# One bias table for the edge blocks, read at offsets, with the row minimum taken in two steps

## The chip, the cores and the metric

The kernel runs on one core of a Trainium2 chip. The metric is device time in microseconds (us), the median of several executions; before the change it is 943.72 us over 3 executions (942.9 to 944.77). One execution was recorded by the hardware profiler, and all durations below come from it.

Engine names: PE is the matrix engine, PEld its weight loads, DVE the vector engine, ACT the scalar engine, POOL the GpSimd engine, SP the engine that issues the DMAs here. DMAs are issued in order from SP's queue.

## The reference: what is computed

One layer of an encoder block over 2 sequences (256 and 2048 tokens of 1024 numbers), with the same 16 learned meta tokens ahead of each. All in float32:

- h = rmsnorm(z), then one projection h @ w_in into q (8 heads of 64), k and v (2 key/value heads), an attention gate, and the value, gate and output gate of a convolution group.
- The convolution group: a gated product, a depthwise convolution of width 31, a layer norm over channels, SiLU.
- The attention group: each real query sees all 16 meta keys without a distance penalty, and the real keys at distance up to 128 with the penalty slope × distance (ALiBi); every softmax row has a learned sink logit besides.
- out = z + concat(attention × SiLU(gate), convolution × SiLU(gate)) @ w_out; the meta tokens are dropped from the output.

The part that the change touches is the score of a block of queries:

```
s = (q @ k^T) * scale - slope * |t - s|      # real keys within 128, else -inf
s_meta = (q @ k_meta^T) * scale              # no penalty
p = softmax([sink, s_meta, s])
```

The row's maximum (here: the minimum of the negated scores, with the negated sink as the starting value) is needed before the exponential.

## The kernel before, in words

Tokens are cut into 18 blocks of 128 (blocks 0 and 1 are the short sequence, 2 to 17 the long one). The work runs in two stages that overlap at their border.

**Projection, norm, convolution (to about 605 us).** PE multiplies in float32r with operands split in a high and a low part, three passes for each product (`proj_et` L856 and `proj_te` L873). The convolution's taps run on DVE. `ln_block` (L211) does the layer norm of the convolution for one block: PE transposes (`lnt`), DVE takes statistics and writes the tile `zn` (L234), PE transposes back (`lnu`, L240), ACT applies SiLU into `zn` (L243), and a DMA stores `zn` as `cd` (L246). `zn` has three buffers, so the write at L234 waits until the store of three blocks ago has landed.

**Attention and output projection.** `attention_open` (L255) allocates a pool on the right side of the on-chip memory. In it are `bias` (128 partitions × 2 × 3040 bf16 before), two key windows `kw`, three score tiles `sb`, the value tiles, `q` (two buffers before) and `q2`. It loads `q` of block 0, the keys, the bias table (L269) and the values. From there the work is cut in slots: `slot_step` (L625), eight slots for each block. In slot 0 of block a the `q` and keys of block a+1 are loaded (`load_q` L327, `load_k` L295), in slot 3 its values; in slot 6 `q_prep` (L392) transposes the `q` of block a+1 on PE (tile `qT`) into `q2`. Each slot has one `scores` (L410), for a key/value head kv and a quarter n of 32 queries × 4 heads:

- PE: two matmuls into the PSUM tile S (L427);
- one slot later `bias_max` (L434): DVE adds the bias to S, writes `sb` and takes the row minimum into a column of `nm`, in one tensor_tensor_reduce (L441), which the profile shows as a CUSTOM_DVE_ANT_0 and a DVE_READ_ACCUMULATOR2_ANT. POOL clears the columns of `sb` that this quarter does not see (L440);
- two slots later `expo`: ACT takes the exponential with `nm` as its offset (L453);
- three slots later, for n = 3, `norm`: DVE forms the reciprocal sums (`es`, L465 and L466), POOL multiplies `sb` by them (L470 for the meta columns of edge blocks, L479).

In the next eight slots `bank` (L491) transposes `sb` on PE (tiles pT_c, pT_m, pT_x), ACT and DVE split it (L515, L516), `pv` multiplies by the values (tile O, L533), `merge` joins and gates the halves (L555 to L566, tile `rest`). `outproj` (L601) does the output projection, six matmuls of 512 columns in each slot (L609), and `yo` is added and stored.

A block is of one of three kinds (L290). Blocks 0 and 2 are "first", 1 and 17 are "last"; these four are the edge blocks, whose window lacks one side. The other 14 are "in". SPANS (L61) gives the columns that a quarter uses: 304 or 336 of an "in" block, 176, 208, 240 and 272 for the four quarters of an edge block. Before, KEYS and BIAS_AT (L66 to L76) lay out one stretch of the bias table for each kind and quarter: 1248 columns for "in", 896 for "first", 896 for "last", 3040 in all, with zeros under the meta keys.

**What sets the order.** The kernel gives a program order, with work put off by so many slots (`later`, `tick`). `TileContext(schedule_with_timeline_sim=True)` (L1310) lets the framework choose the order on each engine's queue from its own estimate of the times. From `attention_open` on, POOL keeps the program order (MAN1, L261); from `attention_rest` (L679) on, PE does too (MAN2, L683). SP, ACT and DVE stay with the framework throughout. The first 14 slots, block 0 and six slots of block 1, run among the last 18 q projections (`spread`, L658), where PE's order is the framework's too. Waits between engines, and for buffers that are used again, are put in by the framework.

Of the kernel before, what the change touches and what calls it, by code (L numbers as in the profile page):

```python
# [11 lines left out]
F32 = mybir.dt.float32  # L12
# [3 lines left out]
ALU = mybir.AluOpType  # L16
AX = mybir.AxisListType

P = 128
D = 1024  # L20
ND = D // P
NM = 16
# [14 lines left out]
BIG = 1.0e30  # L37
# [20 lines left out]
QB = 32  # L58
QC = P // 2
LA, MA, CC, LB, RA, MB, RB, KW = 0, 64, 80, 208, 272, 336, 352, 416  # L60
SPANS = {  # L61
    "in": ((LA, RA + QB), (LA + QB, MB), (CC, RB + QB), (CC, KW)),
    "first": tuple((MA, LB + QB * (n + 1)) for n in range(4)),
    "last": tuple((CC + QB * n, RB) for n in range(4)),
}
KEYS = {  # L66
    "in": ((LA, MA, -P), (MA, CC, None), (CC, LB, 0), (LB, RA, QC - P), (RA, MB, P), (MB, RB, None), (RB, KW, P + QC)),
    "first": ((MA, CC, None), (CC, MB, 0)),
    "last": ((CC, MB, -P), (MB, RB, None)),
}  # L70
BIAS_AT = {}
BIAS_N = 0
for _kind, _spans in SPANS.items():
    for _n, (_c0, _c1) in enumerate(_spans):
        BIAS_AT[_kind, _n] = BIAS_N - _c0
        BIAS_N += _c1 - _c0  # L76
XR = QC + NM
PIN_X = 7
PIN_W = 2
# [20 lines left out]
def hymba_kernel(  # L100
# [11 lines left out]
    nc = tc.nc  # L112
# [22 lines left out]
    snk, msk, nsnk = vec[:, 22:24], vec[:, 24:28], vec[:, 28:30]  # L135
# [26 lines left out]
    def later(k, f):  # L162
        due.setdefault(clock[0] + k, []).append(f)
# [86 lines left out]
    pool, cst, kw, wo, wo_slot, sbs = {}, {}, [], {}, {}, []  # L250
    vt, qt, q2t, sbt, pmt, gat, gct, cnt, mix, att, yot, opj = ({} for _ in range(12))
# [38 lines left out]
    def kind(b):  # L290
        return "first" if b in (0, NB_P) else "last" if b in (NB_P - 1, NB - 1) else "in"

    vt, qt, q2t, sbt, pmt, gat, gct, cnt, mix, att, yot, opj = ({} for _ in range(12))
# [31 lines left out]
        nc.sync.dma_start(t[3][NM:XR], vd[b + 1, QC:P])  # L325

    def load_q(b):  # L327
        qt[b] = pool["a"].tile([P, 4, P], F32, tag="q", name=f"q{b}")
        nc.sync.dma_start(qt[b].rearrange("p a e -> p (a e)"), qd[b])

    def presplit_wo(e):
# [48 lines left out]
    def pin(on):  # L380
        def wrap(f):
            def g(*a, **k):
                r = f(*a, **k)  # L383
                if on:
                    tc.keep_in_program_order(r)
                return r

            return g

        return wrap  # L390
# [19 lines left out]
    def scores(b, kv, n):  # L410

        c0, c1 = SPANS[kind(b)][n]
        w = c1 - c0
        if n == 0:
            sbt[b, kv] = sbs[(2 * b + kv) % 3]
            stat[b, kv] = (
                pool["a"].tile([P, 4], F32, tag="nm", name=f"nm{b}_{kv}", bufs=3),
                pool["a"].tile([P, 4], F32, tag="rs", name=f"rs{b}_{kv}", bufs=3),
                pool["a"].tile([P, 4], F32, tag="es", name=f"es{b}_{kv}", bufs=3),
            )  # L420
        sb = sbt[b, kv]
        nm, rs, es = stat[b, kv]
        ps = psum.tile([P, 512], F32, tag="a", name=f"S{b}_{kv}_{n}")
        for hl_k in range(2):
            pin(b == 0 and hl_k == 0)(
                nc.tensor.matmul)(
                ps[:, 0:w],  # L427
                q2t[b][:, n, 2 * kv : 2 * kv + 2].rearrange("p a c q -> p (a c q)"),
                kw[b % 2][:, kv, hl_k, c0:c1],
                start=(hl_k == 0),  # L430
                stop=(hl_k == 1),
            )

        def bias_max():  # L434
            at = BIAS_AT[kind(b), n]
            z0, z1 = {"in": (0, 0), "first": (c1, MB), "last": (CC, c0)}[kind(b)]
            if n == 0 and b == NB_P + 1:
                z0, z1 = c1, MB
            if z1 > z0:
                nc.gpsimd.memset(sb[:, n, z0:z1], 0.0)  # L440
            nc.vector.tensor_tensor_reduce(  # L441
                out=sb[:, n, c0:c1],
                in0=ps[:, 0:w],
                in1=cst["bias"][:, kv, at + c0 : at + c1],
                scale=1.0,
                scalar=nsnk[:, kv : kv + 1],
                op0=ALU.add,
                op1=ALU.min,
                accum_out=nm[:, n : n + 1],
            )  # L450

        def expo():
            nc.scalar.activation(  # L453
                sb[:, n, c0:c1],
                sb[:, n, c0:c1],
                AF.Exp,
                bias=nm[:, n : n + 1],
                scale=-1.0,
                accum_out=rs[:, n : n + 1],
            )  # L460
            if n == 3:
                nc.scalar.activation(es, nm, AF.Exp, bias=snk[:, kv : kv + 1])

        def norm():
            nc.vector.tensor_tensor(es, es, rs, op=ALU.add)  # L465
            nc.vector.reciprocal(es, es)  # L466
            if kind(b) != "in":
                pm = pool["a"].tile([P, 2, 4, NM], F32, tag="pm", name=f"pm{b}_{kv}", bufs=1)
                at = MA if kind(b) == "first" else MB
                nc.gpsimd.tensor_tensor(  # L470
                    pm,
                    sb[:, :, at : at + NM].unsqueeze(1).to_broadcast([P, 2, 4, NM]),
                    es.unsqueeze(1).unsqueeze(3).to_broadcast([P, 2, 4, NM]),
                    op=ALU.mult,
                )
                pmt[b, kv] = pm
            for k in range(4):
                a0, a1 = SPANS[kind(b)][k]
                nc.gpsimd.tensor_scalar(  # L479
                    sb[:, k, a0:a1], sb[:, k, a0:a1], es[:, k : k + 1], 1.0, op0=ALU.mult, op1=ALU.mult  # L480
                )

        later(1, bias_max)
        later(2, expo)
        if n == 3:
            later(3, norm)
# [214 lines left out]
    if True:  # L701
# [491 lines left out]
        for i, (c, u, g) in enumerate(items):  # L1193
# [25 lines left out]
            for k in loads.get(i, []):  # L1219
# [3 lines left out]
                for q in range(4):  # L1223
                    at = max(1, min(room, W0 + q * min(WST, max(1, (room - 2) // 4))))
# [27 lines left out]
def layout(inputs):  # L1252
    f = {k: np.asarray(v) for k, v in inputs.items()}
    z = np.concatenate([f["meta_tokens"], f["x_prompt"][0], f["x_sample"][0]], axis=0)
    zt = np.ascontiguousarray(z.T).reshape(ND, P, COLS)
    w = f["w_in"][0]
    q, k, v, ga, cv, cg, gc = np.split(w, np.cumsum([512, 128, 128, 512, 512, 512])[:6], axis=1)
    units = []
    for j in range(NJ):
        units.append(np.concatenate([cg[:, P * j : P * j + P], cv[:, P * j : P * j + P]], axis=1))  # L1260
    units += [gc[:, :UW], gc[:, UW:], q[:, :UW], q[:, UW:], np.concatenate([k, v], axis=1), ga[:, :UW], ga[:, UW:]]
    w_in = np.stack([u.reshape(ND, P, UW).transpose(1, 0, 2) for u in units])
    col = lambda a, n: a.reshape(n, P).T
    vecs = np.concatenate(
        [
            col(f["norm_w"][0], 8),
            col(f["conv_b"][0], 4),
            col(f["conv_ln_w"][0], 4),
            col(f["conv_ln_b"][0], 4),
            np.tile(f["q_norm_w"][0], 2)[:, None],  # L1270
            np.tile(f["k_norm_w"][0], 2)[:, None],
        ],
        axis=1,
    )
    conv_w = f["conv_w"][0].reshape(TAPS, NJ, P).transpose(2, 1, 0)
    row = np.arange(P)
    local = row // QB
    sink = np.stack([f["sink_logits"][0][4 * kv + local] for kv in range(KV)], axis=1)
    slopes = np.exp2(-8.0 * np.arange(1, H + 1, dtype=np.float32) / H).astype(np.float32)
    bias_c = np.zeros((P, KV, BIAS_N), np.float32)  # L1280
    for kv in range(KV):
        for (kind, n), at in BIAS_AT.items():
            for c0, c1, key0 in KEYS[kind]:
                a0, a1 = max(c0, SPANS[kind][n][0]), min(c1, SPANS[kind][n][1])
                if key0 is None or a1 <= a0:
                    continue
                key = key0 + np.arange(a0, a1) - c0
                dist = np.abs(key[None, :] - (QB * n + row % QB)[:, None]).astype(np.float32)
                bias_c[:, kv, at + a0 : at + a1] = np.where(
                    dist <= P, slopes[4 * kv + local][:, None] * dist, np.float32(BIG)  # L1290
                )
    mask = ((np.arange(P)[:, None] // NM) % 4 == np.arange(4)[None, :]).astype(np.float32)
    w_out = f["w_out"][0].reshape(8, P, D)
    vecs = np.concatenate([vecs, sink, mask], axis=1)
    bias_c = bias_c.astype(ml_dtypes.bfloat16)
    arrs = dict(z=z, zt=zt, w_in=w_in, w_out=w_out, vecs=vecs, conv_w=conv_w, bias_c=bias_c)
    return {k: np.ascontiguousarray(v) for k, v in arrs.items()}
# [17 lines left out]
```

## Time and profile before

| | |
|---|---|
| median of 3 executions | 943.72 us (942.9 to 944.77) |
| the profiled execution's own time | 943.95 us |
| its span, first to last instruction | 941.9 us |
| so around the span | 2.05 us |
| DVE busy | 744.4 us (79%) |
| ACT busy | 421.8 us (45%) |
| POOL busy | 293.3 us (31%) |
| granted PE clock | 1.000 |
| DMA moved | 176.49 MB, mean 187 GB/s |

The span is the time from the first to the last instruction. Busy time is the union of an engine's instructions. PE's matmuls are pipelined and their ends are modelled, so that a matmul's duration is longer than the distance to the next one's start; only an idle time that the profile names is a sure stop of PE. A timeline row is: start in us, duration in us, engine, line, operation, tiles written <- read, shape, count, and in brackets the idle time ahead of it with what ended it. A row of the stretch view is: stretch, its length, then busy us (count) for PE, PEld, DVE, ACT, POOL, the granted clock, the DMA engines' busy share and GB/s. A row of the chain of waits is: start, length, what. A row of the view of who waited is: who <- for whom: us in total, times, longest.

### The profile page before, as it was taken

The page shows a single profiled execution, that of the slowest core. Times are in us where ns is not written, and L with a number is a line of the kernel's source. Part 1 is how long each engine was busy: PE and PEld are TensorE (multiplying, and loading weights), DVE is VectorE, ACT ScalarE, POOL GpSimd, SP SyncE. Part 2 cuts the span into 40 slices and gives each one's busy share as a digit, 9 for nine tenths or more (in the row PEclk, how much of TensorE's full clock was granted, in tenths as well). Part 3 has the DMA queues.
Part 4 walks back from the last instruction along what each step waited for, and adds up shares of the span by engine and source line. Part 5 has one row for each costly group of instructions (what it writes and reads, how often), then busy time and mean ns, then how long its engine had stood idle before and what let it go on. Part 6 is the DMA issues. An engine that isn't in the chain of part 4 may idle for free.

```text
span 941.9 us, 16665 instructions
## 1 busy us (share of the span) xinstructions
PE 935.6 (99%) x5794; PEld 886.3 (94%) x5794; DVE 744.4 (79%) x1263; ACT 421.8 (45%) x1160; POOL 293.3 (31%) x490
## 2 busy tenths in 40 slices
PE   9999999999999999999999999999999999999998
PEld 8999999999999999999999999988888888888887
DVE  5579999997977879999996655677777677767773
ACT  7432022253457751011111356666666666656661
POOL 4320000173558400000000553755433242333332
PEclk9999999999999999999999999999999999999999
DMA  8575345676656595233333697975666556655512
GB/s 306 170 253 217 134 176 176 217 269 251 182 185 189 182 312 182 90 113 134 140 128 123 159 327 225 395 240 159 200 188 172 151 165 196 188 159 148 163 62 68
DMA packets 146211, 176.49 MB, mean 187 GB/s; under 512 B 40816, under 2 KB 108736, under 8 KB 146000
## 3 DMA queue, kind: packets, MB, share of 16 engines
q1 hardware_dynamic: 146128, 175.43, 57.8%
q8 instruction: 46, 0.75, 0.3%
q14 instruction: 37, 0.30, 0.1%
HBM read 112.69 MB, written 62.70 MB: 186 GB/s over the span
## 4 chain that ended last, share of the span: by engine, by line
PE 94%; DMA 2%; DVE 1%; SPq 1%; issue 0%; ACT 0%; POOL 0%; DVEq 0%; ACTq 0%; POOLq 0%
PE pj L863 43%; PE y L609 21%; PE pj L879 13%; PE O L533 5%; PE S L383 4%; PE pT_c L499 2%; PE pT_m L499 2%; PE pT_x L499 1%; DMA cd<-zn 1%; DMA bias<-in_bias_c 1%; PE qT L383 1%; PE lnu L240 0%; DMA xn<-in_z 0%; PE lnt L221 0%; DVE xt L772 0%
## 5 line engine op out<-in xcount | busy, mean ns | idle before, releaser
L863 PE MATMUL pj<-xh,ws 128*128 128x384 f32 (+1 forms) x1536 | 395.9, 338 | 0.1
L946 DVE SCALAR_TENSOR_TENSOR y<-us,cw,y 128x1167 f32<-128x1167 f32 x240 | 329.0, 1427 | 0.4
L863 PEld LDWEIGHTS pj<-xh,ws 128*128 128x128 f32 x1536 | 280.0, 188 | 0.4 <-ACT xh L1111 0.4
L863 PE MATMUL pj<-xl,ws 128*128 128x384 f32 (+1 forms) x768 | 260.9, 340 | 0.1
L609 PE MATMUL y<-wo,rest 128*128 128x512 f32 (+1 forms) x672 | 172.7, 394 | 0.0
L879 PE MATMUL pj<-ws,xh 128*128 128x256 f32 (+1 forms) x880 | 164.2, 284 | 0.3 <-DVE kn L1037 0.3
L863 PEld LDWEIGHTS pj<-xl,ws 128*128 128x128 f32 x768 | 144.1, 188 | 0.5 <-DVE xl L801 0.4
L609 PEld LDWEIGHTS y<-wo,rest 128*128 128x128 f32 x672 | 117.5, 189 | 21.4 <-DVE rest L566 0.3
L879 PEld LDWEIGHTS pj<-ws,xh 128*128 128x128 f32 (+1 forms) x880 | 136.1, 187 | 1.1 <-issue 0.4
L879 PE MATMUL pj<-ws,xl 128*128 128x256 f32 (+1 forms) x440 | 124.3, 283 | 0.0
L441 DVE CUSTOM_DVE_ANT_0 sb<-S,bias,vec 128x304 f32<-128x304 f32 (+5 forms) x144 | 74.5, 517 | 33.8 <-PE S L383 31.5
L453 ACT ACTIVATE sb<-sb,nm 128x304 f32<-128x304 f32 (+5 forms) x144 | 77.8, 540 | 48.9 <-DVE nm L441 48.2
L971 ACT ACTIVATE go<-pj 128x384 f32<-128x384 f32 x48 | 23.5, 489 | 149.8 <-PE pj L863 142.3
L879 PEld LDWEIGHTS pj<-ws,xl 128*128 128x128 f32 (+1 forms) x440 | 82.2, 187 | 0.2
L479 POOL TENSOR_SCALAR sb<-sb,es 128x304 f32<-128x304 f32 (+5 forms) x144 | 73.1, 525 | 16.0 <-DVE es L466 13.1
L561 POOL TENSOR_TENSOR at<-at,ga 128x256 f32<-128x256 f32 x36 | 26.5, 737 | 164.0 <-DVE at L555 104.8
L148 POOL TENSOR_SCALAR ssk<-ssk 128x2 f32<-128x2 f32 x18 | 8.4, 465 | 210.0 <-ACT sqk L985 210.0
L383 PEld LDWEIGHTS S<-kw,q 128*128 128x128 f32 x288 | 53.2, 188 | 10.6
L383 PE MATMUL S<-kw,q 128*128 128x304 f32 (+5 forms) x288 | 62.8, 299 | 0.0
L148 POOL TENSOR_SCALAR ssq<-ssq 128x4 f32<-128x4 f32 (+2 forms) x55 | 23.5, 427 | 98.3 <-ACT xn L726 74.4
L906 ACT ACTIVATE sg<-pj 128x384 f32<-128x384 f32 (+1 forms) x24 | 11.8, 492 | 82.9 <-PE pj L863 82.0
L609 PE MATMUL y<-wo,mch 128*128 128x512 f32 x144 | 47.2, 409 | 0.0
(139 smaller groups left out, 1306.9 us busy)
## 6 DMA issues: line engine op xcount, KB each, us to landing
wd<-ws SPq DMA_DIRECT2D x36, 512.0 KB, 5.8
ws<-wd SPq DMA_DIRECT2D x36, 512.0 KB, 6.2
wraw<-in_w_in SPq DMA_DIRECT2D x52, 256.0 KB, 6.3
xn<-in_z SPq DMA_DIRECT2D x18, 512.0 KB, 5.5
gd<-go SPq DMA_DIRECT2D x48, 192.0 KB, 2.2
yo<-in_z SPq DMA_DIRECT2D x36, 256.0 KB, 3.9
out_y<-yo SPq DMA_DIRECT2D x35, 256.0 KB, 2.7
wo<-wod SPq DMA_DIRECT2D x16, 512.0 KB, 7.4
```

What stands on the lines that cost most here:

```text
L148: nc.gpsimd.tensor_scalar(src, src, scale, eps, op0=ALU.mult, op1=ALU.add)
L383: r = f(*a, **k)
L441: nc.vector.tensor_tensor_reduce(out=sb[:, n, c0:c1], in0=ps[:, 0:w], in1=cst["bias"][:, kv, at + c0 : at + c1], scale=1.0, scalar=nsnk[:, ...
L453: nc.scalar.activation(sb[:, n, c0:c1], sb[:, n, c0:c1], AF.Exp, bias=nm[:, n : n + 1], scale=-1.0, accum_out=rs[:, n : n + 1],)
L479: nc.gpsimd.tensor_scalar(sb[:, k, a0:a1], sb[:, k, a0:a1], es[:, k : k + 1], 1.0, op0=ALU.mult, op1=ALU.mult)
L499: nc.tensor.transpose(pt[: c1 - c0, n, :], sbt[b, kv][:, n, c0:c1], ident)
L533: nc.tensor.matmul(opj[b, kv][:, n0:n1], t[:r, kv, :], p[:r, n0:n1], start=(k == "c" and i == 0), stop=(k == "x" and i == len(work) - 1),)
L561: nc.gpsimd.tensor_tensor(at[:, pr, :], at[:, pr, :], gat[b][:, pr, :], op=ALU.mult)
L609: nc.tensor.matmul(ps, mh[mi][:, e % 4, :], wo[e, wi][:, cols], start=(e == 4 and k == 0), stop=(e == 3 and k == 2),)
L863: nc.tensor.matmul(ps[:, :n], ws[:, d, wi, P * half_i : P * half_i + P], x[xi][:, d, o : o + n], start=(k == 0), stop=(k == 3 * ND - 1),)
L879: nc.tensor.matmul(ps[:rows, :UW], x[xi][:, d, o : o + rows], ws[:, d, wi, :], start=(k == 0), stop=(k == 3 * ND - 1),)
L946: nc.vector.scalar_tensor_tensor(y[:, yo + o0 : yo + o1], u[:, o0 + k : o1 + k], cw[:, j, k : k + 1], y[:, yo + o0 : yo + o1], op0=ALU.mul ...
```

## The change

Three edits. First, the "first" and "last" stretches of the bias table go. In their place one table of 288 columns holds the penalty for relative positions −128 to 159 (EDGE_AT). An edge quarter's keys read it at an offset that depends on the quarter ("first") or from its start ("last"). The table shrinks from 3040 to 1536 columns, that is from 12160 to 6144 bytes a partition. Second, since the meta keys have no place in that table, an edge quarter takes its minimum in two operations: first the 16 meta columns, with a stretch of zeros of the "in" table as bias and the negated sink as starting value, into a new one-column tile `nx`; then the other columns, with `nx` as the starting value, into `nm`. The 32 edge quarters (4 blocks × 2 heads × 4) so have 64 of these operations in place of 32. The POOL memset stands behind them in the text. Third, `q` has one buffer in place of two. The "in" blocks keep their operation and their bias columns.

```diff
-KEYS = {
-    "in": ((LA, MA, -P), (MA, CC, None), (CC, LB, 0), (LB, RA, QC - P), (RA, MB, P), (MB, RB, None), (RB, KW, P + QC)),
-    "first": ((MA, CC, None), (CC, MB, 0)),
-    "last": ((CC, MB, -P), (MB, RB, None)),
-}
-BIAS_AT = {}
+KEYS = ((LA, MA, -P), (CC, LB, 0), (LB, RA, QC - P), (RA, MB, P), (RB, KW, P + QC))
+BIAS_AT = []
 BIAS_N = 0
...
+for _c0, _c1 in SPANS["in"]:
+    BIAS_AT.append(BIAS_N - _c0)
+    BIAS_N += _c1 - _c0
+EDGE_AT = BIAS_N
+BIAS_N += 2 * P + QB
...
     def load_q(b):
-        qt[b] = pool["a"].tile([P, 4, P], F32, tag="q", name=f"q{b}")
+        qt[b] = pool["a"].tile([P, 4, P], F32, tag="q", name=f"q{b}", bufs=1)
...
         def bias_max():
-            at = BIAS_AT[kind(b), n]
+            def biased(a0, a1, at, first, acc):
+                nc.vector.tensor_tensor_reduce(
+                    out=sb[:, n, a0:a1],
+                    in0=ps[:, a0 - c0 : a1 - c0],
+                    in1=cst["bias"][:, kv, at : at + a1 - a0],
+                    scale=1.0,
+                    scalar=first,
+                    op0=ALU.add,
+                    op1=ALU.min,
+                    accum_out=acc,
+                )
+
+            sink, out_n = nsnk[:, kv : kv + 1], nm[:, n : n + 1]
+            if kind(b) == "in":
+                biased(c0, c1, BIAS_AT[n] + c0, sink, out_n)
+            else:
+                first = kind(b) == "first"
+                m0 = MA if first else MB
+                k0, k1 = (CC, c1) if first else (c0, MB)
+                part = pool["a"].tile([P, 1], F32, tag="nx", name=f"nx{b}_{kv}_{n}", bufs=2)
+                biased(m0, m0 + NM, BIAS_AT[0] + MA, sink, part)
+                biased(k0, k1, EDGE_AT + (P - QB * n if first else 0), part, out_n)
             z0, z1 = {"in": (0, 0), "first": (c1, MB), "last": (CC, c0)}[kind(b)]
...
             if z1 > z0:
                 nc.gpsimd.memset(sb[:, n, z0:z1], 0.0)
-            nc.vector.tensor_tensor_reduce(
-                out=sb[:, n, c0:c1],
-                in0=ps[:, 0:w],
-                in1=cst["bias"][:, kv, at + c0 : at + c1],
-                scale=1.0,
-                scalar=nsnk[:, kv : kv + 1],
-                op0=ALU.add,
-                op1=ALU.min,
-                accum_out=nm[:, n : n + 1],
-            )
...
+        for n, at in enumerate(BIAS_AT):
+            for c0, c1, key0 in KEYS:
...
+        bias_c[:, kv, EDGE_AT:] = alibi(np.arange(-P, P + QB))
```

More of the change, by code (lines that the diff above doesn't have):

```diff
@@ L65 @@
 }
-KEYS = {
-    "in": ((LA, MA, -P), (MA, CC, None), (CC, LB, 0), (LB, RA, QC - P), (RA, MB, P), (MB, RB, None), (RB, KW, P + QC)),
-    "first": ((MA, CC, None), (CC, MB, 0)),
-    "last": ((CC, MB, -P), (MB, RB, None)),
-}
-BIAS_AT = {}
-BIAS_N = 0
[L73 to L76, printed above, removed]
+KEYS = ((LA, MA, -P), (CC, LB, 0), (LB, RA, QC - P), (RA, MB, P), (RB, KW, P + QC))
+BIAS_AT = []
+BIAS_N = 0
+for _c0, _c1 in SPANS["in"]:
[3 more added lines that the diff above has]
+BIAS_N += 2 * P + QB
 XR = QC + NM
@@ L1281, in layout, with alibi @@
     for kv in range(KV):
[L1282 to L1291, printed above, removed]
+        def alibi(rel):
+            dist = np.abs(rel[None, :] - (row % QB)[:, None]).astype(np.float32)
+            return np.where(dist <= P, slopes[4 * kv + local][:, None] * dist, np.float32(BIG))
+        for n, at in enumerate(BIAS_AT):
+            for c0, c1, key0 in KEYS:
+                a0, a1 = max(c0, SPANS["in"][n][0]), min(c1, SPANS["in"][n][1])
+                if a1 > a0:
+                    bias_c[:, kv, at + a0 : at + a1] = alibi(key0 + np.arange(a0, a1) - c0 - QB * n)
+        bias_c[:, kv, EDGE_AT:] = alibi(np.arange(-P, P + QB))
     mask = ((np.arange(P)[:, None] // NM) % 4 == np.arange(4)[None, :]).astype(np.float32)
```

## The prediction

> **What bounds the kernel now.** I read the page's totals first, then the view of equal stretches, then the chain of waits and the timelines around the one place where the stretches show PE stopping.
>
> ```profile
> span 941.9 us, 16665 instructions
> PE 935.6 (99%) x5794; PEld 886.3 (94%) x5794; DVE 744.4 (79%) x1263; ACT 421.8 (45%) x1160; POOL 293.3 (31%) x490
> ```
> ```profile
> 540.00:560.00 20.00, 20.00 (x174) 20.00 (x173) 12.16 (x36) 9.77 (x28) 11.80 (x31) 1.00 0.94 320
> 560.00:580.00 20.00, 19.30 (x164) 18.91 (x164) 9.24 (x20) 11.28 (x32) 8.23 (x20) 1.00 0.73 231
> 580.00:600.00 20.00, 20.00 (x169) 19.83 (x169) 11.58 (x41) 12.28 (x38) 10.63 (x24) 1.00 0.99 342
> 600.00:620.00 20.00, 20.00 (x126) 17.55 (x126) 14.70 (x43) 13.76 (x40) 13.78 (x30) 1.00 1.04 377
> 920.00:940.00 20.00, 18.69 (x109) 16.12 (x107) 6.99 (x14) 3.31 (x7) 4.93 (x8) 1.00 0.22 73
> ```
>
> PE is busy for 935.6 of 941.9 us. The change takes no matmul away, so in all it can win at most the 6.3 us in which PE stands still, and most of that lies at the kernel's start and end. Where the attention opens (540 to 620 us, the first column behind the length is PE) PE is idle in one stretch only, 20.00 − 19.30 = 0.70 us. In the same stretches the DMA engines are loaded to 0.73 to 1.04 of their time (the last but one column). So this is a stage in which PE sets the pace and the DMAs run just behind it. The idle time is one wait:
>
> ```profile
> 574.29 0.28 PE L879 MATMUL pj<-ws,xh 128*128 128x256 f32 x1
> 575.22 0.63 PE L240 MATMUL lnu<-ident,zn 128*128 128x128 f32 x4 [0.66 <-DVE zn L234]
> ```
> ```profile
> 574.27 0.81 DVE L234 TENSOR_SCALAR zn<-lnt,mv 128x512 f32<-128x512 f32 x1 [4.00 <-DMA cd<-zn]
> ```
> ```profile
> 568.34 1.50 ACT L243 ACTIVATE zn<-lnu,vec 128x128 f32<-128x128 f32 x4 [0.69 <-PE lnu L240]
> ```
> ```profile
> 570.19 0.42 SPq L324 DMA_DIRECT2D vb<-vmd  x1
> 570.72 1.75 SPq L246 DMA_DIRECT2D cd<-zn  x1
> ...
> 574.23 0.40 SPq L329 DMA_DIRECT2D q<-qd  x1
> ```
> ```profile
> 552.29 9.46 DMA bias<-in_bias_c
> ...
> 570.72 3.42 DMA cd<-zn
> ```
> ```profile
> SPq L317 <- DMA bias<-in_bias_c: 2.0, 1, 2.0
> ```
>
> Read backwards: PE waits for `zn`, DVE waits 4.00 us for the store of an older `zn` to free its buffer, that store is ready when ACT ends at 568.34 + 1.50 = 569.84, but SP issues it at 570.72, behind loads of later blocks. SP had been held up 2.0 us at L317 by the view of SP's waits, until the bias table, 9.46 us under way, had landed at 561.75. So the bias load is on the path through SP, not through its reader: the first reader starts at 579.81 (below), 18 us after the landing.
>
> **The bias table.** 128 × (12160 − 6144) bytes = 0.77 MB less. At the 320 GB/s of the stretch in which it moves, that is 2.4 us less work for the DMA engines. SP can then run up to 2.0 us (the wait) earlier, but the `cd` store cannot be issued before 569.84, that is 0.88 us earlier. PE stood ready at 574.29 + 0.28 = 574.57 and began at 575.22. Moving `zn` by 0.88 us covers this: the gain is the 0.66 us of the wait, and no more, since behind it PE's next matmul was ready. Bounds: 0 (SP fills the freed time with other loads, the store keeps its place) to 0.7 (all the idle time of that stretch). I take 0.66.
>
> **The second operation in the edge blocks.**
>
> ```profile
> L441 DVE CUSTOM_DVE_ANT_0 sb<-S,bias,vec 128x336 f32<-128x336 f32 x28 | 15.9, 568 | 20.6 <-PE S L383 20.2
> ...
> L441 DVE DVE_READ_ACCUMULATOR2_ANT nm<- 128x1 f32 x144 | 11.9, 82 | 0.0
> ...
> L441 DVE CUSTOM_DVE_ANT_0 sb<-S,bias,vec 128x176 f32<-128x176 f32 x8 | 3.2, 397 | 2.7 <-PE S L383 2.6
> ```
> ```profile
> 579.81 0.40 DVE L441 CUSTOM_DVE_ANT_0 sb<-S,bias,vec 128x176 f32<-128x176 f32 x1
> 580.13 0.08 DVE L441 DVE_READ_ACCUMULATOR2_ANT nm<- 128x1 f32 x1
> ...
> 734.25 0.16 DVE L465 TENSOR_TENSOR es<-es,rs 128x4 f32<-128x4 f32 x1
> 734.45 0.18 DVE L466 RECIPROCAL es<-es 128x4 f32<-128x4 f32 x1
> ```
>
> From 176 to 336 columns the mean grows by 568 − 397 = 171 ns, 1.07 ns a column; 16 columns would take 397 − 160 × 1.07 = 226 ns. The other operation loses 16 columns, 17 ns, and there is one accumulator read more, 82 ns: busy time +291 ns for each of the 32 quarters, 9.3 us in all. What DVE loses in time is a little less, since the accumulator read begins before the operation's end: 176 columns hold DVE from 579.81 to 580.13, 0.32 us, so 16 columns hold it 0.15 us, plus 0.08 us, less 0.02 us for the narrower partner: 0.21 us. The partner reads what the accumulator read has just written, and so starts only after it. The nearest such pair of rows, L465 and L466, starts 0.20 us apart with 0.16 us of work: 0.04 us. So 0.25 us a quarter, between 0.21 (no wait) and 0.33 (both at full length, and the wait). A block has 8 quarters: 2.0 us, 1.7 to 2.6.
>
> [...]
>
> Who waits behind it? ACT's exponential of the same quarter comes 0.25 us later. Whether that reaches PE goes by how full DVE is while the edge blocks run:
>
> ```profile
> 579.50:592.00 12.50, 12.50 (x110) 12.50 (x108) 7.77 (x29) 9.12 (x29) 5.33 (x13) 1.00 0.89 303
> 592.00:612.50 20.50, 20.50 (x152) 19.24 (x151) 13.67 (x40) 12.91 (x39) 14.97 (x31) 1.00 1.06 394
> 612.50:630.50 18.00, 18.00 (x99) 15.10 (x98) 13.80 (x39) 10.66 (x29) 10.63 (x23) 1.00 0.84 260
> 720.00:739.24 19.24, 19.24 (x110) 16.71 (x109) 14.38 (x38) 12.12 (x32) 6.94 (x11) 1.00 0.60 168
> 896.00:915.00 19.00, 19.00 (x112) 16.44 (x111) 13.22 (x38) 10.66 (x30) 7.59 (x18) 1.00 0.22 70
> ```
>
> These are, in order, the bias operations of blocks 0, 1 and 2, a whole "in" block, and block 17; DVE is the third busy number. Block 2 is the fullest: 13.80 of 18.00 us, 4.20 us free. With 8 × 0.29 = 2.3 us more it is 16.1, 90%. It still fits. The chain that is due soonest there is `norm` of the first head:
>
> ```profile
> 622.15 0.17 DVE L466 RECIPROCAL es<-es 128x4 f32<-128x4 f32 x1
> ```
> ```profile
> 623.99 0.40 POOL L470 TENSOR_TENSOR pm<-sb,es 128x128 f32<-128x128 f32 x1 [3.18 <-PE pT_x L495]
> 624.49 1.74 POOL L479 TENSOR_SCALAR sb<-sb,es 128x176 f32<-128x176 f32 x4
> ```
> ```profile
> 627.85 0.60 PE L499 MATMUL pT_c<-ident,sb 128*128 128x128 f32 x4
> ```
>
> DVE is done at 622.32, POOL starts at 623.99 because it waits for PE, is done at 626.23, and PE reads at 627.85. DVE may be 1.67 us late before POOL notices, and 3.3 us before PE does. The first head's four quarters add 1.0 us. I put this edit at 0 us, covered by DVE's 4.20 free us; without that cover it costs up to 2.6 us a block.
>
> POOL's memset stands behind the operations in the text, but is the only POOL work there, so POOL's order is the same; its columns are others than those that DVE writes: nothing.
>
> **One buffer for `q`.**
>
> ```profile
> 553.99 0.43 SPq L329 DMA_DIRECT2D q<-qd  x1
> ```
> ```profile
> 571.14 0.60 PE L383 MATMUL qT<-ident,q 128*128 128x128 f32 x4
> ...
> 582.40 0.60 PE L383 MATMUL qT<-ident,q 128*128 128x128 f32 x4
> ...
> 608.01 0.60 PE L383 MATMUL qT<-ident,q 128*128 128x128 f32 x4
> ```
> ```profile
> DMA to landing us min/median/max: 2.8/4.0/9.1
> ```
>
> Before, the `q` of block 1 was fetched at 553.99. With one buffer it has to wait until block 0's transposes have read theirs, 571.14 + 0.60 = 571.74, and must land by 582.40: 10.7 us for a transfer of 2.8 to 9.1 us (the landing line is that of L329). The row at 574.23 above is `q` of block 2, which waited for that same event with two buffers; were block 1's in its place, it would land at 577.0 to 583.3, at the median 578.2. So 0 us, at the worst 0.9. All later gaps are longer (582.40 to 608.01 is the next; an "in" block lasts 19.24 us). What is queued behind the waiting load on SP are the other loads of the same block and the stores of `zn`; that is the second rival.
>
> **Sum.** Against the profiled execution: 943.95 − 0.66 + 0 + 0 = 943.29 us (span 941.2 and the 2.05 around it). The median of the three runs lies 0.23 below the profiled one: 943.06. For PE's order among the last projections, which the framework chooses anew from its estimates, I add 0.14, a fifth of the 0.70 us idle: 943.2 us.
>
> About 0.2%, 1.9 us, is what a measurement of this kernel can tell from no change: below 941.8 is faster, above 945.6 slower.
>
> **Rivals.**
>
> 1. *The stall stays or moves.* SP uses the time for loads that were next, and the store of `zn` is issued where it was, or another `zn` waits instead. For: loads like that at 570.19 stand ahead of the store. Against: they do not need the store's data, and SP would only issue them earlier too. Gain 0: 943.7.
>
> 2. *The single `q` buffer holds SP.* If the load of block 1's `q` is put ahead of a `zn` store and waits until 571.74, the store that was issued at 570.72 goes at 571.74 + 0.40 = 572.1, 1.4 us later, and PE's 0.66 us wait becomes 2.1. Decides: that load's place on SP relative to that store. For: both fall within a microsecond. Against: with two buffers the load that waited for the same event, at 574.23, stood 3.5 us behind that store. 943.72 + 1.4 = 945.1.
>
> 3. *DVE becomes the bound in the edge blocks (slower).* Mechanism: each quarter's two operations make the queue behind them late, until `norm` reaches PE. It decides when DVE is over 3.3 us late in blocks 1, 2 or 17. Price: 8 × 0.33 = 2.6 us a block at most when nothing hides it, 7.9 us for the three; a third to a half of that if the free time takes the rest: 2.6 to 4.0 us, so 946.3 to 947.7. For: 90% load in block 2, and POOL is busier there than in an "in" block. Against: the 4.20 us.
>
> 4. *More than the stall goes.* With 2.4 us less DMA work all idle time from 540 to 620 us goes and the end of the kernel gains too. 0.7 us plus a like amount at the end, whose stretch idles 1.31 us: 941.7. Nothing at 920 us is tied to the bias table.
>
> That the table shrinks and that 32 quarters get a second operation is certain from the code.
>
> **How the numbers follow.** Forecast (stall gone, rest covered) 0.50; rival 1 0.24; rival 2 0.13; rival 3 0.09; rival 4 0.04. The likeliest is 943.2. Low end 942.3: the sum of 943.06 less the scatter of the three runs (943.72 − 942.9 = 0.8). High end 945.8: rival 2 with half of the 0.9 us of a late `q` and some scatter; rivals 3 and 4 lie outside, 0.13. Faster is rival 4, 0.04; slower is rival 3 and a sixth of rival 2, 0.11; the rest is 0.85.
>
> **What would show it.** Right: one bias landing in about half the time; PE idle in 560 to 580 us below 0.3; 64 edge operations at L441's new line, 32 of them of 16 columns at 0.2 to 0.25 us; DVE busy about 9 us higher; PE still without idle from 580 to 920 us. Wrong: PE waiting for `zn`, `q` or `sb` in those stretches for over 1 us, or `norm` on POOL waiting for DVE rather than PE in block 2.

## The result, and the profile after

The changed kernel takes 947.36 us (median of 6 executions, 946.3 to 948.11) against 944.03 us for the kernel before in 6 executions beside it (942.9 to 944.77). The ratio is 1.0037, 95% interval 1.0024 to 1.005: it is slower by about 3.3 us, where 943.2 us and no change were forecast. The profiled execution took 946.3 us, the lowest of the six, so its trace shows 2.35 us of the loss against the 943.95 us of the execution profiled before. Of one kernel below (e16) two executions were disturbed and are left out of its median and range.

The page's totals of the kernel after:

```profile
span 944.5 us, 16759 instructions
PE 938.2 (99%) x5794; PEld 888.3 (94%) x5794; DVE 750.2 (79%) x1327; ACT 423.1 (45%) x1160; POOL 296.5 (31%) x490
```

DVE has 64 instructions more, the 32 new operations and their accumulator reads, but its busy time rose only by 5.8 us (750.2 − 744.4), where the prediction looked for about 9: the new reads lie for the most part inside the time of their operations, as the rows of the pair further down show. The span is 2.6 us longer and PE's busy time 2.6 us. A busy PE does not prove that no time is lost: at the stop near 606 us, below, the profile names 0.54 us of idle PE, while the distance of the starts, 0.94 us where 0.23 is usual, shows 0.71 us lost. So the distances between starts are used.

Four rows place the 2.6 us. First the first projection matmuls on PE's timeline, before and then after; then PE's transposes of `q` (tile qT) in blocks 3 to 16, before and after, whose numbers behind the colon are shortest/median/longest duration in ns and the times of the first and the last:

```profile
12.20 0.63 PE L863 MATMUL pj<-xh,ws 128*128 128x400 f32 x2
```
```profile
13.11 0.63 PE L871 MATMUL pj<-xh,ws 128*128 128x400 f32 x2
```
```profile
L383 PE MATMUL qT<-ident,q x56: 271/273/273, 643.3 to 893.5; 128*128 128x128 f32 x56
```
```profile
L380 PE MATMUL qT<-ident,q x56: 270/272/273, 645.0 to 896.0; 128*128 128x128 f32 x56
```

Against before, after is 0.9 us late by 12 us, 1.7 by 643 and 2.5 by 896. The first 0.9 us lies in the start-up, 560 us ahead of the first edge block. In the traces of the other kernels below it lies anywhere from 0 to 1.0 us (these matmuls start at 12.21 us in e3 and at 13.13 in e5; 1.0 us late in e14, which is the kernel before with a wider tile), so it is a scatter of the executions and not the change. What is left is +0.8 us between 13 and 643 us and +0.8 over blocks 3 to 16, where no edge block runs at all. Setting the starts of the two traces side by side, matmul for matmul, takes the first of these apart: PE wins 1.1 us between 565 and 575 us, where the stall stood that the prediction wanted to remove, and loses 0.9 by 618 us, with the stop near 606, and 0.9 more by 637, with the stop near 620. The stretches, in the columns of the rows shown before:

```profile
560.00:580.00 20.00, 20.00 (x174) 20.00 (x173) 10.73 (x29) 12.60 (x33) 9.59 (x22) 1.00 0.65 204
600.00:620.00 20.00, 19.41 (x121) 16.70 (x119) 14.84 (x57) 12.94 (x38) 12.52 (x27) 1.00 0.99 348
620.00:640.00 20.00, 19.57 (x102) 16.30 (x103) 16.59 (x50) 12.74 (x35) 12.53 (x25) 1.00 0.55 165
```

The 0.70 us of idle PE in 560 to 580 us is gone. In its place PE is idle for 0.59 and 0.43 us in 600 to 640 us, which had no idle time before. The view of who waited names these stops:

```profile
PE O L541 <- DVE ptiles L524: 0.5, 1, 0.5
PE y L617 <- ACT rest L573: 0.3, 1, 0.3
...
PE y L617 <- DVE rest L574: 0.2, 1, 0.2
```

In PE's timeline they lie near 606 and 620 us:

```profile
605.23 0.40 PE L541 MATMUL O<-ptiles,vc 128*128 128x512 f32 x1
606.17 0.50 PE L541 MATMUL O<-ptiles,vc 128*128 128x512 f32 x1 [0.54 <-DVE ptiles L524]
...
620.24 0.73 PE L617 MATMUL y<-wo,rest 128*128 128x512 f32 x2 [0.29 <-ACT rest L573]
621.17 1.19 PE L617 MATMUL y<-wo,rest 128*128 128x512 f32 x4 [0.19 <-DVE rest L574]
```

By starts, the first stop costs 0.94 us from one matmul to the next where 0.23 is usual.

**The stop near 606 us** goes with another order of PE's own matmuls. Before, PE transposes `sb` (pT_c, pT_m) until 602 us, then runs the last projection matmuls, and only then turns to O:

```profile
601.99 0.27 PE L499 MATMUL pT_m<-ident,sb 128*128 128x128 f32 x1
602.02 0.36 PE L879 MATMUL pj<-ws,xh 128*128 128x256 f32 x1
...
604.82 0.28 PE L879 MATMUL pj<-ws,xh 128*128 128x256 f32 x1
604.94 0.39 PE L383 MATMUL S<-kw,q 128*128 128x240 f32 x2
605.16 0.40 PE L533 MATMUL O<-ptiles,vc 128*128 128x512 f32 x1
```

After, the projection matmuls come first and the transposes right ahead of O, so that DVE's `ptiles`, which O reads, ends only at 605.43 + 0.69 = 606.12 us (an edge pair stands ahead of it on DVE, but the stop is there in kernels without pairs too, below):

```profile
603.53 0.28 PE L887 MATMUL pj<-ws,xh 128*128 128x256 f32 x1
603.65 0.60 PE L507 MATMUL pT_c<-ident,sb 128*128 128x128 f32 x4
```
```profile
605.43 0.69 DVE L524 TENSOR_TENSOR ptiles<-pT_c,ptiles 128x512 fp32r<-128x512 f32 x1
```

The text of the kernel asks for no such change: PE's order among the last projections is the framework's.

**The stop near 620 us** can be followed through three engines. These are POOL's rows of the kernel before, in block 1, second head: the multiplication of the meta columns (`norm`), of the others, and the gate's multiplication `at` of `merge`:

```profile
615.22 0.40 POOL L470 TENSOR_TENSOR pm<-sb,es 128x128 f32<-128x128 f32 x1 [3.16 <-PE pT_x L495]
615.72 1.73 POOL L479 TENSOR_SCALAR sb<-sb,es 128x272 f32<-128x272 f32 x4
617.42 0.74 POOL L561 TENSOR_TENSOR at<-at,ga 128x256 f32<-128x256 f32 x1
```

The same three after:

```profile
616.82 0.40 POOL L478 TENSOR_TENSOR pm<-sb,es 128x128 f32<-128x128 f32 x1 [4.09 <-DVE es L474]
617.32 1.74 POOL L487 TENSOR_SCALAR sb<-sb,es 128x272 f32<-128x272 f32 x4
619.01 0.74 POOL L569 TENSOR_TENSOR at<-at,ga 128x256 f32<-128x256 f32 x1
```

ACT's next row, before and then after:

```profile
618.20 0.41 ACT L565 CAST rest<-at 128x256 fp32r<-128x256 f32 x1 [0.37 <-POOL at L561]
```
```profile
619.78 0.40 ACT L573 CAST rest<-at 128x256 fp32r<-128x256 f32 x1 [0.97 <-POOL at L569]
```

`norm` waits for DVE's `es`, done at 616.64 in place of 613.91 us: in DVE's queue the edge pairs stand ahead of it (e3 below, without the second operations, does not have this stop). `at` stands behind `norm` in POOL's queue, although it needs nothing of it, and so starts 1.6 us later; ACT's and DVE's halves of `rest` follow it, and PE needs them for the output projection. Before, the next matmuls of the output projection began at 618.98, 0.37 us after ACT's row had ended: that was all the slack there was.

The new pair on DVE itself, in its timeline:

```profile
578.41 0.23 DVE L433 CUSTOM_DVE_ANT_0 sb<-S,bias,vec 128x16 f32<-128x16 f32 x1
578.56 0.08 DVE L433 DVE_READ_ACCUMULATOR2_ANT nx<- 128x1 f32 x1
578.68 0.39 DVE L433 CUSTOM_DVE_ANT_0 sb<-S,bias,nx 128x160 f32<-128x160 f32 x1
```

The partner starts 0.27 us after the first operation, 0.04 us after the accumulator read has ended (578.64).

### The profile page after: what moved, and what is told of

The parts are those of the page before. It is cut to its first block, busy times and chain, and to the rows that moved or that the text cites. A ratio compares the mean times of both kernels' runs of the same rounds, so it can differ in the third digit from the quotient of the medians.

```text
span 944.5 us, 16759 instructions
## 1 busy us (share of the span) xinstructions
PE 938.2 (99%) x5794; PEld 888.3 (94%) x5794; DVE 750.2 (79%) x1327; ACT 423.1 (45%) x1160; POOL 296.5 (31%) x490
## 4 chain that ended last, share of the span: by engine, by line
PE 97%; DVE 1%; DMA 1%; SPq 0%; issue 0%; ACT 0%; DVEq 0%
PE pj L871 43%; PE y L617 21%; PE pj L887 16%; PE O L541 5%; PE S L380 4%; PE pT_c L507 2%; PE pT_m L507 2%; PE pT_x L507 1%; PE lnt L218 1%; PE lnu L237 1%; PE qT L380 1%; DMA wraw<-in_w_in 1%; DVE xt L780 0%; PE kt L1055 0%; SPq L837 0%
## 5 line engine op out<-in xcount | busy, mean ns | idle before, releaser
L433 DVE CUSTOM_DVE_ANT_0 sb<-S,bias,vec 128x304 f32<-128x304 f32 (+2 forms) x144 | 67.5, 469 | 35.3 <-PE S L380 34.2
L145 POOL TENSOR_SCALAR ssq<-ssq 128x4 f32<-128x4 f32 (+2 forms) x55 | 25.4, 463 | 94.1 <-ACT xn L734 72.8
```

The costliest lines, as they stand in the source:

```text
L145: nc.gpsimd.tensor_scalar(src, src, scale, eps, op0=ALU.mult, op1=ALU.add)
L433: nc.vector.tensor_tensor_reduce(out=sb[:, n, a0:a1], in0=ps[:, a0 - c0 : a1 - c0], in1=cst["bias"][:, kv, at : at + a1 - a0], scale=1.0, ...
```

## The experiments

Theory A: the second operations are the loss, through POOL's queue (the stop near 620 us). Theory B: the single `q` buffer is, through SP's queue. Theory C, for the 0.8 us in blocks 3 to 16: the new tile `nx`, two buffers of one column, is laid above `kw`, `sb`, `vc`, `vm`, `q2`, `nm`, `rs` and `es` and moves them 64 bytes down, and PE then goes at another pace. No view of the profile shows the addresses: the 64 bytes are the author's assumption, and e8, in which a tile is 64 bytes wider by its text, has the period of the changed kernel. The order of instructions there is the same on PE, DVE, ACT and POOL, and PE has no idle time. For C, "period" is the mean distance of the same matmul in successive "in" blocks of one trace: 19.241 us before, 19.296 after. The third decimal depends on the matmuls that are averaged; by the transposes of `q` alone it is 19.241 and 19.301.

**e1: only the single q buffer** (943.88 us, 11 executions; ratio to the kernel before 1.0004, 0.9995 to 1.0013).

```diff
-        qt[b] = pool["a"].tile([P, 4, P], F32, tag="q", name=f"q{b}")
+        qt[b] = pool["a"].tile([P, 4, P], F32, tag="q", name=f"q{b}", bufs=1)
```

> The kernel before, with q in one buffer and nothing else changed; PE, DVE, ACT and POOL keep their order, SP's alone differs. Theory A (the second operation makes DVE and with it POOL late, and PE stops twice between 600 and 625 us) expects no change: within 0.5 us of before, PE idle 0.66 us at 574 as before. Theory B (the single q buffer costs a little in each of the 14 inner blocks, 0.06 us each by the difference of the two traces from 640 to 910 us) expects +0.8 us, as a drift over that stretch.

No effect, and theory B falls. Its stretches show more than its time:

```profile
560.00:580.00 20.00, 20.00 (x174) 20.00 (x173) 9.94 (x23) 11.86 (x32) 9.17 (x21) 1.00 0.69 218
600.00:620.00 20.00, 19.52 (x120) 16.76 (x119) 14.43 (x43) 13.79 (x40) 12.96 (x29) 1.00 1.03 373
```

The stall of 560 to 580 us is gone with the long table in place, and 0.48 us of idle PE stands in 600 to 620 us instead, at 602 us and for ACT's `sqq` (squares of a projection's result). The same time, the stop elsewhere.

**e2: only the two operations and their tile `nx`, on the long table, q double** (947.02 us, 5 executions; 1.0037, 1.0023 to 1.005).

```diff
-            nc.vector.tensor_tensor_reduce(
-                out=sb[:, n, c0:c1],
...
+                biased(m0, m0 + NM, sink, part)
+                biased(k0, k1, part, out_n)
```

> The kernel before, with the edge quarters' minimum in two operations on the old long table; q keeps two buffers. Theory A expects most of the loss here: +1.5 to +3 us, with PE waiting for DVE and ACT between 600 and 625 us, and the 0.66 us wait near 574 us still there since the long table is loaded. Theory B expects +0.5 us or less.

A loss as large as the whole one comes with this edit, with the period at 19.296 us and the stops of PE for `ptiles` (0.6 us) and for `rest` (0.3 and 0.2 us).

**e3 and e9: the changed kernel with one operation in each edge quarter,** over the meta columns too, which then read the penalty's table where zeros are wanted; e3 with one `q` buffer, e9 with two.

```diff
-                biased(m0, m0 + NM, BIAS_AT[0] + MA, sink, part)
-                biased(k0, k1, EDGE_AT + (P - QB * n if first else 0), part, out_n)
+                biased(c0, c1, EDGE_AT + (P - QB * n - NM if first else 0), sink, out_n)
```

> The changed kernel with one operation in an edge quarter: it reads the short table 16 columns further left or right, so that the meta keys get a penalty from the table instead of zero (this part of the computation is altered). Short table and single q buffer stay. Theory A expects before minus the 0.66 us wait: 0 to -1 us against before, no PE wait for DVE or ACT between 600 and 625 us. Theory B expects the drift of 0.8 us to be there, so about +0.2 us. A third theory C (the shifted addresses of the tiles slow the inner blocks) expects the drift here too.

> The changed kernel with one operation in an edge quarter (the meta keys get a penalty from the table instead of zero) and two buffers for q, so that the short table alone is left. With one buffer for q this came out 2.1 us slower than before in the timed runs, though the profiled run was not slower. If the single buffer does that, this is within 0.7 us of before; if the short table or the order that comes with it does, it is again +2 us.

e3: 945.54 us (11 executions; 1.0023, 1.0014 to 1.0031), e9: 944.59 us (11; 1.0009, 1.0 to 1.0017). This edit leaves out the tile `nx` too. The periods are 19.240 and 19.239 us and nothing stops at 620 us, so the slower period and this stop come with the second operations and their tile. PE still waits for `ptiles` near 605 us, 0.5 and 0.4 us, though theory A expected no such wait in e3: this stop does not need a second operation. And neither kernel is back at the time before; e3 is 2.1 us above it. e3's profiled execution, 943.82 us, was the lowest of its eleven by 1 us; the trace does not show where the others lost 1.7 us. e9's trace has two stops of PE by the distance of starts, 0.56 us beyond the usual near 565 and again near 605 us, where the kernel before has one of 0.82, near 574.

**e4: the changed kernel with two q buffers** (946.81 us, 5 executions; 1.0034, 1.0022 to 1.0047).

```diff
-        qt[b] = pool["a"].tile([P, 4, P], F32, tag="q", name=f"q{b}", bufs=1)
+        qt[b] = pool["a"].tile([P, 4, P], F32, tag="q", name=f"q{b}")
```

> The changed kernel with two buffers for q; all engines but SP keep the changed kernel's order. Theory A expects the changed kernel's time, +3.3 us against before. Theory B expects +2.5 us, with no drift from 640 to 910 us.

As the changed kernel, drift and stops and all: B falls from the other side.

**e5: norm behind merge on POOL** (946.15 us, 9 executions; 1.0023, 1.0013 to 1.0033).

```diff
-            later(3, norm)
+            later(2, lambda: later(1, norm))
```

> The changed kernel, with norm put behind the merge of the block before in POOL's order (its call is made one step later in the same slot). Theory A2 (PE's stop near 620 us comes from the gate multiply that stands on POOL behind a norm that now waits for DVE) expects that stop gone, about 0.9 us less than the changed kernel, +2.4 us against before. If the stop stays, the gate multiply is not held by norm.

POOL's rows of e5 in the same place:

```profile
616.79 0.74 POOL L569 TENSOR_TENSOR at<-at,ga 128x256 f32<-128x256 f32 x1 [2.73 <-DVE at L563]
617.49 0.40 POOL L478 TENSOR_TENSOR pm<-sb,es 128x128 f32<-128x128 f32 x1
617.99 1.91 POOL L487 TENSOR_SCALAR sb<-sb,es 128x272 f32<-128x272 f32 x4
```

And its stretch there:

```profile
620.00:640.00 20.00, 20.00 (x110) 17.06 (x109) 14.79 (x51) 11.97 (x34) 13.26 (x26) 1.00 0.56 170
```

`at` no longer waits for `norm`, and PE does not stop. By the medians it is 1.2 us below the changed kernel; the two ratios' intervals touch, so the size is rough, but the stop itself went as theory A has it. This trace has the stop near 606 us and, near 574 us, one of 0.8 us, so its profiled execution is no faster than that of the changed kernel.

**e11: the same edit in the kernel before** (943.69 us, 11 executions; 0.9997, 0.9988 to 1.0006).

> The kernel before with norm behind merge on POOL, the edit that took 1.2 us off the changed kernel. If it mends a wait that only the second operations cause, it does nothing here: 943.3 to 944.1 us, no stop near 620 in either. If the order is simply the better one, it beats the kernel before by about 1 us: 942.5.

Nothing: the order on POOL only matters where `es` is late. PE's order among the last projections is another here as well, and the trace has a wait of 0.4 us for `ptiles` at 605 us, with the long table and one operation in each quarter.

**e7: no new tile,** the first minimum in a spare column of `nm`, so that all addresses are as before (947.02 us, 7 executions; 1.0032, 1.002 to 1.0043).

```diff
-                part = pool["a"].tile([P, 1], F32, tag="nx", name=f"nx{b}_{kv}_{n}", bufs=2)
+                part = nm[:, 4 + n : 5 + n]
```

> The changed kernel, with the first minimum in a spare column of nm in place of the new tile nx, so that the addresses of kw, sb, q2 and the values are those of the kernel before. Theory C expects 0.8 us less than the changed kernel, about +2.5 us against before, no drift from 640 to 910 us, and PE's stops between 600 and 625 us still there. The rival expects +3.3 us as in the changed kernel.

The period is 19.242 us, as before the change. The time hardly moved: in its trace PE waits 1.4 us for `zn`, a stop that the changed kernel's trace does not have although every engine has the same order in both. The stops near 606 and 620 us stay.

**e8: the kernel before with its tiles 64 bytes lower,** by a wider `pm` of which nothing more is used; the order is the same on all engines (944.82 us, 11 executions; 1.0009, 1.0 to 1.0018).

```diff
-                pm = pool["a"].tile([P, 2, 4, NM], F32, tag="pm", name=f"pm{b}_{kv}", bufs=1)
+                pm = pool["a"].tile([P, 9 * NM], F32, tag="pm", name=f"pm{b}_{kv}", bufs=1)[:, : 8 * NM].rearrange("p (a h m) -> p a h m", a=2, h=4)
```

> The kernel before, with the tile pm 64 bytes wider and nothing else changed: every engine keeps its order, but the tiles kw, sb, vc, vm, q2, nm, rs and es lie 64 bytes lower, as they do in every kernel that has the new tile nx. Theory C (these addresses make PE slower by 0.06 us in each inner block) expects +0.8 us, as a drift from 640 to 910 us. The rival (the drift comes from the second operations themselves) expects no change.

```profile
L383 PE MATMUL qT<-ident,q x56: 270/272/273, 642.8 to 893.8; 128*128 128x128 f32 x56
```

The transposes span 251.0 us, as in the changed kernel, against 250.2 before: theory C holds, without any second operation. The median rose by the 0.8 us that were expected, with an interval that just reaches down to no change.

**e12 to e15: 128, 192, 256 and 512 bytes,** with `10`, `11`, `12` and `16 * NM` in the same line.

> The kernel before with pm 128 bytes wider, so that kw, sb, vc, vm, q2, nm, rs and es lie 128 bytes lower; with 64 bytes the inner blocks went from 19.241 to 19.296 us. If what counts is where the tiles begin within 128 bytes, 128 restores it: 19.24 us and 943.4 to 944.1 us. If it is their distance from the tiles that do not move, or their distance from pm, the period stays near 19.30 us (or takes a third value) and the time is about 0.8 us higher, 944.5.

> The kernel before with pm 192 bytes wider, so that kw, sb, vc, vm, q2 and the small tiles lie 192 bytes lower. If TensorE's pace goes by where the tiles begin within 256 bytes, 192 is a fourth value between 19.24 and 19.30 us; if the loss grows with every step away from the old place, it is at or above 19.30 us.

> As the last, 256 bytes lower. If the pace goes by the place within 256 bytes, the inner blocks are back at 19.241 us (13 blocks in 250.2 us); if by the distance from the tiles that stay, they are not, and the 13 blocks take 250.7 us or more.

> As the last, 512 bytes lower. Period of 256 or of 512 bytes: 19.241 us, 250.2 us for 13 blocks. If 256 gave another value than the old one and 512 gives the old one, the period is 512; if neither does, there is no simple rule in these steps.

The rows of e13 and of e14:

```profile
L383 PE MATMUL qT<-ident,q x56: 270/272/273, 642.8 to 892.3; 128*128 128x128 f32 x56
```
```profile
L383 PE MATMUL qT<-ident,q x56: 272/273/273, 643.4 to 893.6; 128*128 128x128 f32 x56
```

| bytes lower | first to last qT, us | period, us |
|---|---|---|
| 0 (before) | 250.2 | 19.241 |
| 64 (e8; changed kernel) | 251.0 | 19.296 |
| 128 (e12) | 250.7 | 19.266 |
| 192 (e13) | 249.5 | 19.180 |
| 256 (e14) | 250.2 | 19.243 |
| 512 (e15) | 250.1 | 19.239 |

The first case of e12's expectation, that the place within 128 bytes counts, fell: 128 gave a third value, 19.266 us. 256 and 512 give the first back, so, as far as these steps go, the place within 256 bytes counts; 192 is faster than the old place. In time e12 is level with the kernel before (944.00 us, 11 executions; 0.9998, 0.9989 to 1.0007), where 0.5 us more would follow from its trace; e13 to e15 ran once each (942.66, 944.01 and 943.88 us).

**e17: e13 timed** (943.02 us, 11 executions; 0.9997, 0.9989 to 1.0006).

> The kernel before with pm 192 bytes wider, timed. If the place within 256 bytes sets the pace, the inner blocks take 19.180 us again, 0.06 us less each, 14 to 15 of them: 0.8 to 0.9 us, so 942.8 to 943.2 us and a ratio near 0.9991. If the single fast run was scatter, no difference: 943.9 us.

The period is 19.179 us again, and the profiled execution took 942.66 us, but the ratio's interval holds both a gain of 0.9 us and none: a gain is not shown in the time.

**e6: the changed kernel with its table padded to 3040 columns** (946.52 us, 9 executions; 1.0026, 1.0016 to 1.0036).

```diff
-BIAS_N += 2 * P + QB
+BIAS_N += 1792
```

> The changed kernel with its bias table padded to the old 3040 columns, which no instruction reads beyond the short one. If the short table is what took the 0.66 us stall near 574 us, as the prediction had it, the stall and SP's 2.0 us wait come back and the time goes to about 948.0 us. If the stall comes and goes with the order that the framework gives SP's queue, as the kernel before with a single q buffer suggests (stall gone, table long), the time stays at 947.0 to 947.6 us.

SP's wait for the table in e6, and then in the changed kernel:

```profile
SPq L300 <- DMA bias<-in_bias_c: 2.0, 1, 2.0
```
```profile
SPq L300 <- DMA bias<-in_bias_c: 1.7, 1, 1.7
```

With twice the table SP waits 0.3 us longer, PE does not wait for `zn` in either, and the time is not higher. The size of the table did not matter.

**e10: both repairs, e5 and e7 together** (945.27 us, 11 executions; 1.0012, 1.0003 to 1.0021).

> The changed kernel without its new tile (the first minimum goes to a spare column of nm, so that kw, sb and the others keep their old addresses) and with norm put behind merge on POOL. If the loss is two separate things, POOL's queue near 620 us and the shifted addresses from 640 us on, both are gone: no wait of PE for DVE's or ACT's rest near 620, the period of the inner blocks 19.24 us, and a time about 1.1 + 0.8 us below the changed kernel's 947.4, so 945.0 to 945.8; what is left over the kernel before is the stop near 606 us. If the second operation costs time wherever it stands, the time stays at 946.8 to 947.4.

```profile
PE lnu L237 <- DVE zn L231: 1.3, 1, 1.3
...
PE O L541 <- DVE ptiles L524: 0.5, 1, 0.5
```

The period is 19.242 us and no stop is left at 620 us; 1.05 us over the kernel before remain, and the trace shows stops at both places, near 573 and near 606 us.

**e16: e10 with two q buffers** (944.82 us, 9 executions, 943.78 to 945.41; 1.0011, 1.0001 to 1.0021). **e18: e16 with the 192 bytes** (943.91 us, 11 executions; 1.0004, 0.9995 to 1.0013).

> The changed kernel with both repairs and two buffers for q; only SP's queue stands in another order. If the stop near 573 us (1.3 us of waiting for zn) comes with that order, it shrinks or goes, and the time is about 944.3 us, at the kernel before; if it comes with the second operations, it stays, and the time is 945.3 us as with one buffer.

> The changed kernel with both repairs, two q buffers and the 192 bytes. The addresses should give 0.8 to 0.9 us against the same kernel without them (944.8 us): 944.0 us, level with the kernel before. If the second operations cost nothing else, it is level with the shifted kernel before, 943.0 us; if they cost about 1 us in the stops near 573 and 605 us, it stays 1 us above that.

e16's trace, an execution of 943.84 us, has only the stop near 605 us and not the one for `zn`, and the time did not follow: the profiled execution was again near the lowest. e18, with the same order on every engine, has both stops again, so the order on SP does not decide on the one for `zn`. It has the period of 19.182 us and is level with the kernel before, but 0.9 us above e17, the kernel before with the same addresses.

## Why the prediction was wrong

**The second operation: its size was right, its cover was not.** The first operation takes 231 ns in the mean (226 were worked out) and the pair is 0.27 us apart (0.25), with the wait of 0.04 us that the prediction took from another pair. What failed is the step "I put this edit at 0 us, covered by DVE's 4.20 free us". It looked at how full DVE was in a stretch, and at one chain, the `norm` of block 2's first head, with 1.67 and 3.3 us of slack. In block 1's second head the work behind `norm` in POOL's queue, `at`, had 0.37 us of slack before PE. e5 shows that path: with `at` ahead of `norm` the stop is gone. The prediction listed `norm` waiting for DVE rather than PE as a sign against it, but named block 2; it was block 1. Rival 3 had the engine, and its price (946.3 to 947.7) holds the measured time, but that is luck in part: its mechanism is the stop near 620 us, 0.9 of the 2.4 us of the trace. Its condition, over 3.3 us late in blocks 1, 2 or 17, was far too generous, and it had 0.09 of the chances.

**The new tile: not in the sum.** The prediction counted the instructions that use `nx`, not that it moves its neighbours. That cost 0.8 us over blocks 3 to 16 in the traces (251.0 against 250.2), at places where the change edits nothing. e8 shows it alone; e10 differs from e5 in the tile alone, and its median is 0.9 us lower, with intervals that overlap.

**The bias table: the 0.66 us went, but not for the reason given.** The stall is absent in the changed kernel, as forecast, also in e6 with the long table and in e1; it is there in e7 and e10 with the short one. So the table does not decide. Nor does the order alone: the changed kernel and e7 have the same order on every engine, and PE stops for 0 and 1.4 us; so it is with e16 and e18, 0 and 1.1 us. The kernels that keep both the order and the long table of the kernel before, moved tiles apart, idle 0.70 us (before), 0.14 (e8), 0.53 (e12), 0.20 and 0.21 (the 192 bytes, twice) and 0 (e14, e15) in 560 to 580 us. The view of who waited has the stall of the kernel before, and then of e13, as:

```profile
PE lnu L240 <- DVE zn L234: 0.7, 1, 0.7
```
```profile
PE lnu L240 <- DVE zn L234: 0.2, 1, 0.2
```

The 0.66 us was thus the size of the stall in one execution and not a cost of the long table. A gain there can be lost again: e1 and e15 have a stop near 602 us in its place. It need not be: e8, e13 and e17 have no later stop and reach block 3 at 642.8 us, 0.5 ahead of the kernel before. What sets the size of the stall stays open.

**PE's order among the last projections: 0.14 us booked.** The prediction added this for the order that the framework chooses anew. Of the 20 kernels, eight have the PE order of the kernel before (it, e1, e8, e12 to e15, e17), and in none of them does PE wait for `ptiles` near 606 us; the other twelve have one of five new orders, and in all of them it waits, 0.4 to 0.7 us, whether they have the second operations or not (e3, e9 and e11 do not). In the changed kernel that stop costs 0.7 us by starts, five times the term.

**One q buffer: 0 us, right.** e1 and e4 show no effect of its own, and in the changed kernel PE does not wait for `q`.

**What stays open.** About 1 us of the 3.3 is left in e10 and e16, with intervals that begin near nothing. It need not be the second operations: e9, without them and without `nx`, has 0.9 us as well, and e3 2.1. In the traces what is left is the wait for `ptiles` near 606 us, which comes with PE's new order, and the stall near 574 us where it is there. No run has the change with PE's old order, so that the order is the cause is read from the traces and not tested. e3's and e16's profiled executions were 1.7 and 1.0 us faster than their medians; what the other executions lost no trace shows.

## What to carry to other kernels

Cover is not free time on an engine in a stretch. For each operation that grows, follow every instruction queued behind its readers on the same engine, here an unrelated multiplication on POOL that started 1.6 us later, to the bound engine, and take the smallest slack. A new tile can move its neighbours; here one of a single column went with 19.296 us for an inner block in place of 19.241. Compare the addresses of what the bound engine reads, and try a pad before blaming an instruction. Where the framework chooses the order, compare the bound engine's order before and after; a change of text elsewhere can alter it. And before the price of a wait is booked as a gain, see in a second execution that it is there, and look for the next wait behind it.

## What the runs showed of the hardware

PE's pace went by where the tiles around it lie, in the traces of this kernel. The "in" blocks, with the same instructions in the same order and a granted clock of 1.00, took 19.241 us each in the kernel before, 19.296 with `kw`, `sb` and their neighbours 64 bytes lower (e8), 19.266 with 128 (e12), 19.180 with 192 (e13), 19.243 with 256 (e14) and 19.239 with 512 (e15), up to 0.6% apart. Single distances between starts change by some nanoseconds: two matmuls of 336 columns of S follow each other in 154 ns in the trace of the kernel before and in 158, by the median, in that of the changed kernel. No run shows the cause, and which of the moved tiles counts was not tried.
